# A hybrid decoder layer: the attention's squares a step later, small PSUM users in the values' bank, silu behind the weight splits, another order at v and at the scans' entry

## The chip, the cores and the metric

One core of one Trainium2 chip runs the whole layer as one program. Its engines are called here as the profile calls them: PE multiplies matrices (PEld is its weight load), DVE, ACT and POOL work on tiles in on-chip memory, SP issues the DMA transfers. The metric is the device time of one execution in microseconds. Matmul results go to PSUM, which is cut into banks; every tile in it belongs to a pool with a fixed number of buffers, and a new tile of a pool waits until the last reader of the buffer that it takes over is done.

## The reference, cut to what matters

Sixteen meta tokens are put ahead of 1024 tokens of 1024 channels. One layer computes a state-space mixer (SSD) and a stick-breaking attention side by side, projects both together, and then runs a feed-forward net with a depthwise convolution:

```python
xn = rms_norm(h, mix_pre_g)
proj = xn @ w_in                      # z, x/B/C, dt, q, k, v
xbc = silu(causal_dwconv(xbc))        # 4 taps
y_ssd = ssd_mixer(z, xbc, dt, ...)    # chunks of 128 tokens, a state passed on
# attention, 16 heads of 64:
zlog = q k^T / 8;  beta = sigmoid(zlog)
A[t,s] = beta[t,s] * prod_{s<j<t} (1 - beta[t,j])      # s < t
y_sb = rms_norm(A v, sb_norm_g)       # over all 1024 channels of a token
h = h + rms_norm(concat(y_ssd, y_sb) @ w_out)
g, u = rms_norm(h) @ w_up;  f = (gelu(causal_dwconv(g)) * u) @ w_down
return h + rms_norm(f)
```

## The kernel before, in words

All products run in a split precision: a float32 operand becomes a high part (ACT, a copy to the matmul's rounded type, `whi`, L181) and a low part (POOL, operand minus high part, `wlo`, L182), and three matmuls stand for one. The large projections use a seven-product scheme of the Strassen kind, so that sums of weight blocks are split as well (`whi4x` is the high part of the sum `s24x`).

The order of PE, DVE, ACT and POOL is the order in which the code emits instructions: the parts that matter here stand in manual schedules. SP's order is that of the DMA calls in the scans and the attention. The stages, with their times in the profile of before:

- Duos (60 to 355 us). Each duo projects two blocks of 128 channels with seven products of about 4 us (matmuls at L308). Behind each product stands a slot, into which the work on the last duo's result is put: for x, B and C four convolution taps on DVE, silu (L501) and skip (L507) on ACT, and turnings to token order in three parts (transposes to `tt_X` at L480/L485, ACT copies to `xtkX` at L481/L486). `done_conv` (L520) says which of it goes into which of the slots 0 to 9. In the same places the next duo's weights are summed and split; `split_4` (`whi4x`, then `wlo4x`) stands just ahead of slot 5.
- v (355 to 438 us). The values by the same scheme, `VORDER` = 1, 2, 6, 7, 5, 4, 3, each product in two halves s = 0, 1 over four token blocks t. The sums of weight blocks (`v_sum`, L792) run on DVE and POOL during product 2, the splits (`vwhi` L727, `vwlo` L728) follow. `v_tail` (L840) adds 64 small matmuls.
- Scans (438 to 595 us). 18 units of the state-space mixer with much waiting between engines. Between their parts the last q and k projections are run as filling (`pj_q`, `pj_k`, L218): `scan_fill` is called 54 times and gives out `SCAN_FILL` steps per 27 calls. A finished q/k piece `st` (three buffers, ACT L921 and DVE L927) is put on a list `stores`; `put_stores` issues what stands on it, and is called when the next piece is finished.
- Attention (595 to 885 us). Eight passes p, one per pair of heads, of four steps m. A step loads q blocks on SP, forms scores `z` (L1279, L1280 sigmoid on ACT), runs the products along the keys as scans on DVE (`kp`, L1285), turns earlier scans (`tw` L1303, ACT copy `th` L1308) and multiplies still earlier ones with the values (`av` L1323, ACT copy to `ysc` L1327). `do` fills in matmuls of the output projection (`mo`, L1471). PSUM pool `zz` has three buffers, shared by z, tw, `twc` (corner transposes, `edge_turn`), `halo` (rows for the output projection) and `pta` (norm sums); pool `av` has one, and uses its columns 0:2, at m = 2 also 2:4.
- At m = 2 of pass p, `edge_mix` closes pass p−1: DVE adds the tail from `av` to `ysc` (L1352), then ACT squares the finished `ysc` (`sqb`, L1359), then POOL adds that to the sum of squares `sq` (L1360). `sqb` takes a `th` buffer. In m = 3 and m = 0, `load_v` fetches the next pass's values and a shifted copy `w` (one buffer); POOL subtracts (L1220) in two parts of 5 and 4 blocks.
- Then the output projection, the feed-forward net, and the final norm (885 to 1697 us).

Of the kernel before, what the change touches and what calls it, by code (L numbers as in the profile page):

```python
# [9 lines left out]
F32 = mybir.dt.float32  # L10
# [3 lines left out]
ALU = mybir.AluOpType  # L14
# [3 lines left out]
P = 128  # L18
# [19 lines left out]
NQA = 4  # L38
SCAN_FILL = 41
FILLS = (4,) + 8 * (2,) + 23 * (1,)  # L40
# [26 lines left out]
def tile_layer(ctx: ExitStack, tc: tile.TileContext, x, meta, rows, parts,  # L67
# [721 lines left out]
    nc.sync.dma_start(out=vdz[0:1], in_=vzero)  # L789
    def v_sum(dst, a, b, op, eng):  # L790
        for s in range(2):
            eng.tensor_tensor(vq[dst][s], vq[a][s], vq[b][s], op=op)  # L792

# [56 lines left out]
    def load_b12():  # L850
        xo["b12"] = x_tile(xp, "bxh", "b12rh"), x_tile(xp, "bxl", "b12rl")
        for t, d in zip(xo["b12"], b12d):
            nc.sync.dma_start(out=t.bitcast(F32), in_=d)

    for a, n in enumerate(VORDER):
        nx = VORDER[a + 1] if n != 3 else None
        for s in range(2):
            for t in range(4):
                v_product(n, t, s)
                if nx is not None and t == (3 * (1 - s) + s if n == 2 else s):  # L860
                    v_split(nx, s)
                if n == 2 and (s, t) == (0, 0):
                    v_tail()
                    v_sum((1, 1), (1, 1), (0, 1), ALU.add, nc.vector)
                    v_sum((0, 1), (0, 0), (0, 1), ALU.subtract, nc.gpsimd)
                    v_sum((0, 0), (1, 1), (0, 0), ALU.subtract, nc.vector)
                if n == 6 and (s, t) == (0, 2):
                    v_sum((1, 0), (1, 0), (0, 0), ALU.subtract, nc.gpsimd)
# [94 lines left out]

    def token_rstd(r, pool, nm, pt):
# [6 lines left out]
        nc.vector.memset(ms[:, 0:1], 1.0)  # L971
        nc.vector.tensor_scalar(ms[:2, 0:1], pt[:2, 0:1], 1.0 / D, EPS, op0=ALU.mult, op1=ALU.add)
        nc.vector.tensor_scalar(ms[:, 1:], pt[:, 1:NT + 1], 1.0 / D, EPS, op0=ALU.mult, op1=ALU.add)
        nc.gpsimd.tensor_tensor(r, ms, nhalf[:, :NT + 1], op=ALU.pow)
# [8 lines left out]
    with tc.tile_pool(name="ssd", bufs=1, side="right") as sp:  # L983
# [171 lines left out]
        nc.sync.dma_start(out=dtk, in_=dtkd)  # L1155
        load_x(*units[0])
        load_bc(*units[1])
# [9 lines left out]
        for n, (g, c) in enumerate(units):  # L1167
            if n == 12:
                for d, u in zip(vcd, (vd, vdp)):
                    nc.sync.dma_start(out=d.rearrange("(t r) c -> t r c", r=NM),  # L1170
                                      in_=u[P:].rearrange("(t r) c -> t r c", r=P)[:, :NM])
            if n in (0, 2, 6, 10):
# [80 lines left out]

    corner = []

# [92 lines left out]
    def edge_mix(p, av):  # L1348
        av = av[:, 2:4].rearrange("p a c -> p (a c)")
        ysc = ys_of.pop(p)  # L1350
        tail = ysc[:, :, 96:P]
        nc.vector.tensor_tensor(tail, av.rearrange("p (t c) -> p t c", c=32), tail, op=ALU.add)  # L1352
        stores.append((yd1[:, :, p, :].rearrange("t d c -> d t c"), ysc))
        flat = ysc.rearrange("p t c -> p (t c)")
        if p == 0:
            nc.scalar.activation(sq[:, NM:L], flat, AF.Square)
        else:
            sqt = ap.tile([P, 2, 4, P], F32, tag="th", name=f"sqb{p}", bufs=4).rearrange("p h b c -> p (h b c)")
            nc.scalar.activation(sqt, flat, AF.Square)  # L1359
            nc.gpsimd.tensor_tensor(sq[:, NM:L], sq[:, NM:L], sqt, op=ALU.add)  # L1360

# [171 lines left out]
    def halo_go(r):  # L1533
        acc = psum_zz(f"halo{r}")[:, 0, 0:256]
        for k in (2 * r, 2 * r + 1):
# [18 lines left out]
    def row():  # L1554
        run(wsteps, 1)

    extras = {(1, 0): lambda: do(4), (1, 2): lambda: load_rows(2), (2, 0): lambda: load_rows(2), (3, 2): lambda: (halo_go(0), row()),
              (4, 0): row, (4, 2): lambda: (halo_go(1), row(), load_rows(2)),
              (5, 0): lambda: (row(), load_rows(2)), (5, 2): load_y0, (6, 0): load_y0, (6, 2): lambda: halo_go(2),
              (7, 0): split_y0, (7, 2): lambda: (halo_go(3), split_y0()), (8, 2): row, (9, 2): row, (10, 2): row,  # L1560
              (11, 2): row}
# [5 lines left out]
    for step in range(4 * 8):  # L1567
# [29 lines left out]
        if p > 0 and m == 1:  # L1597
            edge = edge_turn(p - 1)
        extra(step, 2)
        if p == 7:  # L1600
            run(meta_steps, 1)
        if p == 0 and m == 1:
            run(token_rstd(r_ssd, ap, "a", psum_zz("pta")[:, 0, :]))
    while corner:
        corner_copy(*corner.pop(0))
    pair_mix(*mix.pop(0), psum_av("av32"))
    do(1)
    pair_turn(*turn.pop(0))
    do(4)
    edge = edge_turn(7)  # L1610
    av = psum_av("av33")
    pair_mix(*mix.pop(0), av, (7, edge))
    put_stores()
    run(meta_steps)
# [842 lines left out]
```

## Time and profile before

| | us |
|---|---|
| median of three runs | 1698.51 (1696.07 to 1701.05) |
| the profiled execution | 1699.53 |
| span of its profile | 1697.4 |
| PE busy in the span | 1641.2 (97%) |
| DVE, ACT, POOL busy | 1084.5, 746.4, 765.9 |
| mean granted TensorE clock | 0.989 |

The span is the time from the first to the last instruction in the profile; some 2.1 us of the profiled execution lie around it. In the profile's rows a bracket such as `[1.66 <-ACT th L1308]` behind an instruction says how long its engine stood idle before it and which instruction of which engine ended that wait. PEclk is the clock that TensorE was granted in a window, as a share of full speed. The three stages of the diff's main parts have PE busy for 286.80 of 295 us (60 to 355), 37.96 of 42 (438 to 480), and 152.22 of 160 (710 to 870).

### The profile page before, as it was taken

What the parts mean: (1) busy time and instruction counts of PE and PEld (TensorE: products, weight loads), DVE (VectorE), ACT (ScalarE), POOL (GpSimd) and SP (SyncE); (2) the same over time, 40 slices, a digit from 0 to 9 for tenths busy, and PEclk for the clock granted to TensorE, in tenths of its full rate; (3) what the DMA queues carried; (4) which work ended last, traced back from release to release, by engine and by line L of the source; (5) the groups of instructions that cost most, each with busy time, mean ns of one, the idle gap of its engine ahead of it and who ended that gap; (6) DMA issues with size and microseconds to landing.
All of it is one profiled execution on the core that took longest, in us unless ns stands there. A gap on an engine that the chain in (4) does not pass through costs nothing.

```text
span 1697.4 us, 28962 instructions
## 1 busy us (share of the span) xinstructions
PE 1641.2 (97%) x11508; PEld 1442.9 (85%) x11508; DVE 1084.5 (64%) x1253; ACT 746.4 (44%) x1094; POOL 765.9 (45%) x582
## 2 busy tenths in 40 slices
PE   6899999999999989999999999999999999999998
PEld 5899999987777888878877888999889889888887
DVE  7776644345367678877742378666665656658777
ACT  6444344332144357766644244433333333344544
POOL 3675756620276553344332012776677777300001
PEclk9999999999999999999999999999999999999999
DMA  5333334334487866453426543232222223395335
GB/s 191 145 141 114 126 125 150 126 152 136 145 227 234 257 204 198 121 150 109 125 81 212 168 154 120 91 121 94 93 94 94 94 95 113 115 328 189 99 112 186
DMA packets 164517, 247.38 MB, mean 146 GB/s; under 512 B 18487, under 2 KB 99495, under 8 KB 162702
## 3 DMA queue, kind: packets, MB, share of 16 engines
q1 hardware_dynamic: 164382, 245.53, 44.8%
q8 instruction: 91, 1.49, 0.4%
q14 instruction: 44, 0.36, 0.1%
HBM read 161.99 MB, written 83.46 MB: 145 GB/s over the span
## 4 chain that ended last, share of the span: by engine, by line
PE 81%; issue 6%; DVE 5%; POOL 3%; DMA 2%; ACT 2%; SPq 1%; POOLq 0%; DVEq 0%; ACTq 0%
PE fX L1861 10%; PE mo L1471 10%; PE dnA L2273 7%; PE fY L1861 7%; PE fA L1861 7%; PE dnB L2273 5%; DVE kp L1285 3%; PE av L1323 3%; PE z L1279 3%; PE tw L1303 2%; PE pj_k L218 2%; PE dXqk L308 2%; PE pj_q L218 2%; PE vB L811 2%; PE vA L811 2%
## 5 line engine op out<-in xcount | busy, mean ns | idle before, releaser
L1285 DVE TENSOR_TENSOR_SCAN kp<-kp,hold 128x396 f32<-128x396 f32 (+5 forms) x224 | 197.1, 949 | 43.5 <-ACT kp L1280 41.7
L182 POOL TENSOR_TENSOR wlo<-wr,whi 128x1024 fp32r<-128x1024 f32 x43 | 99.3, 2318 | 41.0 <-ACT whi L181 41.0
L2310 POOL TENSOR_TENSOR fms<-fms 128x1 f32<-128x1 f32 x8 | 2.3, 287 | 222.0 <-DMA ar<-fda 185.9
L181 ACT ACTIVATE whi<-wr 128x1024 fp32r<-128x1024 f32 x43 | 45.7, 1062 | 112.2 <-PE fX L1861 73.5
L1933 DVE SCALAR_TENSOR_TENSOR ga<-gr,pp,ga 128x1024 f32<-128x1024 f32 x44 | 69.2, 1574 | 34.0 <-ACT ga L1926 33.2
L2195 ACT ACTIVATE dh<-ar 128x512 fp32r<-128x512 f32 x77 | 48.6, 631 | 94.8 <-PE dnB L2273 44.7
L1280 ACT ACTIVATE kp<-z 128x788 f32<-128x788 f32 (+4 forms) x96 | 73.6, 835 | 23.6 <-PE z L1279 19.7
L2196 DVE TENSOR_TENSOR dl<-ar,dh 128x512 fp32r<-128x512 f32 x77 | 53.2, 691 | 47.1 <-ACT dh L2195 47.1
L1279 PE MATMUL z<-k,q 64*128 64x396 f32 (+9 forms) x672 | 68.1, 345 | 15.1 <-ACT th L1308 9.7
L1279 PEld LDWEIGHTS z<-k,q 64*128 64x128 f32 x672 | 55.4, 195 | 28.3 <-ACT th L1308 17.5
L1308 ACT ACTIVATE th<-tw 128x1024 f32<-128x1024 f32 (+2 forms) x96 | 70.7, 811 | 14.0 <-PE tw L1303 12.6
L1323 PE MATMUL av<-th,v 128*64 128x128 f32 x1152 | 72.1, 281 | 0.0
L1303 PE MATMUL tw<-ident,kp 128*128 128x128 f32 x576 | 70.0, 276 | 0.5 <-DVE kp L1285 0.5
L1323 PEld LDWEIGHTS av<-th,v 128*64 128x64 f32 x1152 | 64.4, 140 | 6.5 <-issue 4.8
L1303 PEld LDWEIGHTS tw<-ident,kp 128*128 128x128 f32 x576 | 62.4, 141 | 7.5 <-issue 6.3
L2273 PE MATMUL dnA<-dl,dh 128*128 128x512 f32 x176 | 68.6, 390 | 0.0
L2273 PE MATMUL dnA<-dh 128*128 128x512 f32 x176 | 68.6, 390 | 0.0
L2273 PE MATMUL dnA<-dh,dl 128*128 128x512 f32 x176 | 68.5, 389 | 0.0
L1994 POOL TENSOR_TENSOR al<-wr,ah 128x512 fp32r<-128x512 f32 x20 | 28.6, 1429 | 77.6 <-ACT ah L1993 77.5
L1257 POOL TENSOR_SCALAR cb<-kp 128x32 f32<-128x32 f32 x64 | 36.1, 573 | 56.0 <-DVE kp L1285 53.3
L497 DVE SCALAR_TENSOR_TENSOR cdX<-craw_x,pp,cdX 128x1040 f32<-128x1040 f32 x24 | 51.5, 2146 | 0.6
L2273 PE MATMUL dnB<-dl,dh 128*128 128x512 f32 x132 | 51.4, 390 | 0.0
(986 smaller groups left out, 6041.5 us busy)
## 6 DMA issues: line engine op xcount, KB each, us to landing
wr<-in_w_up SPq DMA_DIRECT2D x44, 512.0 KB
fds<-ga SPq DMA_DIRECT2D x44, 256.0 KB
b<-in_w_down SPq DMA_DIRECT2D x44, 256.0 KB
ar<-fds SPq DMA_DIRECT2D x44, 256.0 KB
fda<-ga SPq DMA_DIRECT2D x33, 256.0 KB
ar<-fda SPq DMA_DIRECT2D x33, 256.0 KB
k<-qkd SPq DMA_DIRECT2D x8, 1040.0 KB
q<-qkd SPq DMA_DIRECT2D x64, 128.0 KB
```

The costliest lines, as they stand in the source:

```text
L182: nc.gpsimd.tensor_tensor(l, raw, h.bitcast(F32), op=ALU.subtract)
L218: mm(acc[:, :CQ - s], a[:, k, :], b[:, k % 4, c + s:c + CQ], start=(k == 0 and j == 0), stop=(k == KB - 1 and j == 2))
L1279: mm(z[:, j, a - lo:e - lo], u[h, :], r[h, a - bases[x]:e - bases[x]], start=s_ == 0, stop=s_ == 2)
L1280: nc.scalar.activation(kp[:, :, lo:top], z[:, :, :top - lo], AF.Sigmoid, scale=-QSCALE)
L1285: nc.vector.tensor_tensor_scan(part, part, hold[:, L - last + a:L - last + e][:, ::-1], 1.0 if e == last else kp[:, j, e:e + 1], op0=ALU.m ...
L1303: nc.tensor.transpose(tw[:, j, b, :], kp[:, j, c0:c0 + P], ident)
L1308: copied[0] = nc.scalar.activation(th[:, :, :nb, :], tw[:, :, :nb, :], AF.Copy, scale=-1.0, bias=1.0).ins
L1323: mm(av[halves[j], 1 - x, :], v[:, kb, halves[j]], th[:, j, b, :], start=kb == 0, stop=kb == i)
L1471: recent[0] = mm(acc, u[:, k, :], v[:, cs], start=(k == 0 and j == 0), stop=(k == 7 and j == 2))
L1861: mm(acc[:, c, :nn], u[:, k, :], v[:, k, c0:c0 + nn], start=first and k == 0 and j == 0, stop=k == 3 and j == 2, skip_group_check=not first)
L1933: nc.vector.scalar_tensor_tensor(v, self.g[jj][:, :, i:i + 256], fconv_w[:, j, i:i + 1], v, op0=ALU.mult, op1=ALU.add)
L2273: mm(banks[BANK[n], t], u[:, 0, c], v[:, 1, :], start=(n in (1, 2, 5) and p == 0 and i == 0), stop=(p == NPR - 1 and i == 2), skip_group_c ...
```

## The change

Five places of the code are touched; no arithmetic is added or taken away.

- `done_conv`: silu and skip of the duo's second block go from slot 4 to slot 5.
- v: product 1 takes its token blocks in the order 3, 0, 1, 2; `v_tail` and the sums come one product later, and the sums go half by half (part 0 behind block 1, part 1 behind block 3); the split of product 6's first half comes one block earlier.
- Scan entry: `put_stores` is called before the loads of the second unit and in the first two units; `SCAN_FILL` is 39 instead of 41, and the first unit gets four filling steps of its own (24 matmuls) between its state matmul (`st`, L1101) and its output matmuls (`yt`, L1117); the sum of the steps stays 82.
- Attention, PSUM: `twc`, `halo` and `pta` take columns of the `av` bank instead of a `zz` buffer; two of the four `halo_go` calls come two to four steps later; the first norm's scaling of `pta` runs on ACT, its memset on POOL, both from DVE.
- Attention, order: the square and its sum are put on a list `later` and come out at m = 3, behind that step's value product.

```diff
-SCAN_FILL = 41
+SCAN_FILL, FIRST = 39, 8
...
     def done_conv(duo, blocks):
         (a, ta_), (b, tb_) = (conv_acts(*args) for args in blocks)
-        return [a[:2], a[2:4], a[4:] + b[:2], b[2:4], ta_[:1] + b[4:], ta_[1:2], ta_[2:], tb_[:1], tb_[1:2], tb_[2:]]
+        return [a[:2], a[2:4], a[4:] + b[:2], b[2:4], ta_[:1], ta_[1:2] + b[4:], ta_[2:], tb_[:1], tb_[1:2], tb_[2:]]
...
+    def v_sums(part):
+        v_sum((1, 1), (1, 1), (0, 1), ALU.add, nc.vector, part)
+        v_sum((0, 1), (0, 0), (0, 1), ALU.subtract, nc.gpsimd, part)
+        v_sum((0, 0), (1, 1), (0, 0), ALU.subtract, nc.vector, part)
+
     for a, n in enumerate(VORDER):
         nx = VORDER[a + 1] if n != 3 else None
         for s in range(2):
-            for t in range(4):
+            for t in (3, 0, 1, 2) if n == 1 else range(4):
                 v_product(n, t, s)
-                if nx is not None and t == (3 * (1 - s) + s if n == 2 else s):
+                if nx is not None and t == (2 * (1 - s) + s if n == 2 else s):
                     v_split(nx, s)
-                if n == 2 and (s, t) == (0, 0):
+                if n == 2 and (s, t) == (0, 3):
+                    v_sums(1)
+                if n == 2 and (s, t) == (0, 1):
                     v_tail()
-                    v_sum((1, 1), (1, 1), (0, 1), ALU.add, nc.vector)
-                    v_sum((0, 1), (0, 0), (0, 1), ALU.subtract, nc.gpsimd)
-                    v_sum((0, 0), (1, 1), (0, 0), ALU.subtract, nc.vector)
+                    v_sums(0)
...
-        prev = [None, None]
-        run(fill, 8)
+        run(fill, FIRST - 8)
         cur = chunk_weights(*units[0])
...
+            if n < 2:
+                put_stores()
...
             scan_fill()
+            if n == 0:
+                run(fill, 4)
...
-    def edge_turn(p):
+    def edge_turn(p, av):
         cb = edges.pop(p)
-        tw = psum_zz(f"twc{p}").rearrange("p h (b c) -> p (h b) c", c=P)
+        tw = av[:, 2:4]
...
-        if p == 0:
-            nc.scalar.activation(sq[:, NM:L], flat, AF.Square)
-        else:
-            sqt = ap.tile([P, 2, 4, P], F32, tag="th", name=f"sqb{p}", bufs=4).rearrange("p h b c -> p (h b c)")
-            nc.scalar.activation(sqt, flat, AF.Square)
-            nc.gpsimd.tensor_tensor(sq[:, NM:L], sq[:, NM:L], sqt, op=ALU.add)
+
+        def square():
...
+        later.append(square)
...
     def halo_go(r):
-        acc = psum_zz(f"halo{r}")[:, 0, 0:256]
+        acc = av[:, 2:4].rearrange("p a c -> p (a c)")
...
             pair_mix(*mix.pop(0), av, p > 0 and m == 2 and (p - 1, edge))
+            if m == 3:
+                while later:
+                    later.pop(0)()
```

`square` holds the five removed lines as they were. The `run(fill, 8)` and the `put_stores` that open the scans now stand ahead of `load_bc(*units[1])`, so FIRST − 8 = 0 steps are left behind the loads.

On ACT in the second x duo (`craw_x` and `cdX` are the convolution's input and result, `s24x` a weight sum), before:

```order
L181 ACTIVATE whi1x_1243<-wrx_811 128x8x128
L481 ACTIVATE xtkX_1247<-tt_X_0_1248 16x128
L501 ACTIVATE cdX_1184<-cdX_1184 128x1040
L507 ACTIVATE craw_x_840<-cdX_1184,pp 128x1040
L181 ACTIVATE whi4x_1279<-s24x_1148 128x8x128
L486 ACTIVATE xtkX_1247<-tt_X_1_1283 128x512
L486 ACTIVATE xtkX_1247<-tt_X_2_1314 128x512
```

The same place on ACT after the change:

```order
L181 ACTIVATE whi1x_1243<-wrx_811 128x8x128
L481 ACTIVATE xtkX_1247<-tt_X_0_1248 16x128
L181 ACTIVATE whi4x_1276<-s24x_1148 128x8x128
L486 ACTIVATE xtkX_1247<-tt_X_1_1280 128x512
L501 ACTIVATE cdX_1184<-cdX_1184 128x1040
L507 ACTIVATE craw_x_840<-cdX_1184,pp 128x1040
L486 ACTIVATE xtkX_1247<-tt_X_2_1314 128x512
```

The weight split `whi4x` and one turning copy now stand ahead of silu and skip.

On DVE in v (`vq` are weight blocks and their sums, `vwlo` low parts; numbers 3909 and 3911 are the two halves of one block), before:

```order
L792 TENSOR_TENSOR vq_3909<-vq_3909,vq_3905 128x1024
L792 TENSOR_TENSOR vq_3911<-vq_3911,vq_3907 128x1024
L792 TENSOR_TENSOR vq_3681<-vq_3909,vq_3681 128x1024
L792 TENSOR_TENSOR vq_3683<-vq_3911,vq_3683 128x1024
L728 TENSOR_TENSOR vwlo_4061<-vq_3681,vwhi_4060 128x1024
L728 TENSOR_TENSOR vwlo_4083<-vq_3683,vwhi_4082 128x1024
```

The same six on DVE after the change:

```order
L791 TENSOR_TENSOR vq_3909<-vq_3909,vq_3905 128x1024
L791 TENSOR_TENSOR vq_3681<-vq_3909,vq_3681 128x1024
L728 TENSOR_TENSOR vwlo_4052<-vq_3681,vwhi_4051 128x1024
L791 TENSOR_TENSOR vq_3911<-vq_3911,vq_3907 128x1024
L791 TENSOR_TENSOR vq_3683<-vq_3911,vq_3683 128x1024
L728 TENSOR_TENSOR vwlo_4083<-vq_3683,vwhi_4082 128x1024
```

The first half's low part now comes before the second half's sums.

On POOL in the attention, around m = 2 and m = 3 of a pass (`cb` corner copies, `yl` a split for the output projection, `meta_q` and `meta_k` the meta tokens' rows), before:

```order
L1257 TENSOR_SCALAR cb_8518<-kp_1_8625 128x2x16 x2
L1360 TENSOR_TENSOR sq<-sq,sqb_8777 128x1024
L1457 TENSOR_TENSOR yl_4_8819<-yk_4_8296,yh_4_8818 128x1024
L1257 TENSOR_SCALAR cb_8518<-kp_2_8722 128x2x16 x2
L1225 TENSOR_TENSOR meta_q<-qm_8580 64x2 x2
L1227 TENSOR_TENSOR meta_k<-k_8578 128x16
L1220 TENSOR_TENSOR v_8780<-v_8780,w_0_8783 128x640
L1257 TENSOR_SCALAR cb_8518<-kp_3_8829 128x2x16 x2
```

The same place on POOL after the change:

```order
L1271 TENSOR_SCALAR cb_8510<-kp_1_8617 128x2x16 x2
L1475 TENSOR_TENSOR yl_4_8807<-yk_4_8289,yh_4_8806 128x1024
L1271 TENSOR_SCALAR cb_8510<-kp_2_8713 128x2x16 x2
L1376 TENSOR_TENSOR sq<-sq,sqb_8876 128x1024
L1239 TENSOR_TENSOR meta_q<-qm_8572 64x2 x2
L1241 TENSOR_TENSOR meta_k<-k_8570 128x16
L1234 TENSOR_TENSOR v_8768<-v_8768,w_0_8771 128x640
L1271 TENSOR_SCALAR cb_8510<-kp_3_8817 128x2x16 x2
```

The sum of squares now stands directly ahead of the meta rows and of the values' first subtraction, where it stood a step earlier.

More of the change, by code (lines that the diff above doesn't have):

```diff
@@ L789, in tile_layer, with v_sum @@
     nc.sync.dma_start(out=vdz[0:1], in_=vzero)
-    def v_sum(dst, a, b, op, eng):
-        for s in range(2):
-            eng.tensor_tensor(vq[dst][s], vq[a][s], vq[b][s], op=op)
+    def v_sum(dst, a, b, op, eng, s):
+        eng.tensor_tensor(vq[dst][s], vq[a][s], vq[b][s], op=op)
     def v_tile(key):
@@ L857, in tile_layer @@
         for s in range(2):
[L858 removed]
+            for t in (3, 0, 1, 2) if n == 1 else range(4):
                 v_product(n, t, s)
[L860 removed]
+                if nx is not None and t == (2 * (1 - s) + s if n == 2 else s):
                     v_split(nx, s)
[L862 removed]
+                if n == 2 and (s, t) == (0, 3):
+                    v_sums(1)
+                if n == 2 and (s, t) == (0, 1):
                     v_tail()
[L864 to L866 removed]
+                    v_sums(0)
                 if n == 6 and (s, t) == (0, 2):
[L868 removed]
+                    for part in range(2):
+                        v_sum((1, 0), (1, 0), (0, 0), ALU.subtract, nc.gpsimd, part)
                 if n == 6 and (s, t) == (1, 3):
@@ L962, in tile_layer, with token_rstd @@
     qs = {}
-    def token_rstd(r, pool, nm, pt):
+    def token_rstd(r, pool, nm, pt, scalar=False):
         for t in range(NT + 1):
@@ L970, in token_rstd @@
         ms = pool.tile([P, NT + 1], F32, tag="tms", name=f"tms{nm}")
-        nc.vector.memset(ms[:, 0:1], 1.0)
-        nc.vector.tensor_scalar(ms[:2, 0:1], pt[:2, 0:1], 1.0 / D, EPS, op0=ALU.mult, op1=ALU.add)
-        nc.vector.tensor_scalar(ms[:, 1:], pt[:, 1:NT + 1], 1.0 / D, EPS, op0=ALU.mult, op1=ALU.add)
+        (nc.gpsimd if scalar else nc.vector).memset(ms[:, 0:1], 1.0)
+        for rows_, cols_ in ((slice(0, 2), slice(0, 1)), (slice(0, P), slice(1, NT + 1))):
+            if scalar:
+                nc.scalar.activation(ms[rows_, cols_], pt[rows_, cols_], AF.Copy, scale=1.0 / D, bias=EPS)
+            else:
+                nc.vector.tensor_scalar(ms[rows_, cols_], pt[rows_, cols_], 1.0 / D, EPS, op0=ALU.mult, op1=ALU.add)
         nc.gpsimd.tensor_tensor(r, ms, nhalf[:, :NT + 1], op=ALU.pow)
@@ L1156, in tile_layer @@
         load_x(*units[0])
+        prev = [None, None]
+        run(fill, 8)
+        put_stores()
         load_bc(*units[1])
@@ L1252, in tile_layer @@
     edges, ys_of = {}, {}
-    corner = []
+    corner, later = [], []
     def corner_copy(p, i, kp, m, n):
@@ L1597, in tile_layer @@
         if p > 0 and m == 1:
-            edge = edge_turn(p - 1)
+            edge = edge_turn(p - 1, av)
         extra(step, 2)
@@ L1602, in tile_layer @@
         if p == 0 and m == 1:
-            run(token_rstd(r_ssd, ap, "a", psum_zz("pta")[:, 0, :]))
+            run(token_rstd(r_ssd, ap, "a", psum_av("pta")[:, 0, :], True))
     while corner:
         corner_copy(*corner.pop(0))
-    pair_mix(*mix.pop(0), psum_av("av32"))
+    av = psum_av("av32")
+    pair_mix(*mix.pop(0), av)
     do(1)
@@ L1609, in tile_layer @@
     do(4)
-    edge = edge_turn(7)
+    edge = edge_turn(7, psum_zz("twc7").rearrange("p h (b c) -> p (h b) c", c=P))
     av = psum_av("av33")
     pair_mix(*mix.pop(0), av, (7, edge))
+    later.pop(0)()
     put_stores()
```

12 lines of the change are left out of this document (10 added, 2 removed).

## The prediction, made before the changed kernel was run

> **What bounds the kernel now.** The page comes first: span, busy shares, and the chain of work that ended last.
>
> ```profile
> span 1697.4 us, 28962 instructions
> PE 1641.2 (97%) x11508; PEld 1442.9 (85%) x11508; DVE 1084.5 (64%) x1253; ACT 746.4 (44%) x1094; POOL 765.9 (45%) x582
> PE 81%; issue 6%; DVE 5%; POOL 3%; DMA 2%; ACT 2%; SPq 1%; POOLq 0%; DVEq 0%; ACTq 0%
> ```
>
> PE is busy 97% of the span and carries 81% of the chain. The change leaves PE's matmuls as they are, so it can only win idle time of PE, some 56 us in all, or time at a lowered clock. The second view is therefore PE's waits, grouped by waiting line and releaser; only the rows of places that the diff touches are shown.
>
> ```profile
> PE z L1279 <- ACT th L1308: 9.7, 6, 2.0
> PE dXx L308 <- POOL wlo4x L182: 2.5, 2, 1.3
> PE yt L1117 <- DVE em L1081: 1.9, 1, 1.9
> PE tt_X L480 <- ACT xtkX L486: 1.4, 3, 0.7
> PE vB L811 <- DVE vwlo L728: 1.3, 1, 1.3
> PE dXqk L308 <- POOL wlo4qk L182: 1.2, 1, 1.2
> PE z L1279 <- PE z L1279: 1.1, 2, 0.8
> PE vA L811 <- DVE craw_qk L320: 0.9, 1, 0.9
> PE halo L1537 <- ACT th L1308: 0.7, 1, 0.7
> PE dXz L308 <- POOL wlo4z L182: 0.5, 1, 0.5
> PE z L1279 <- DVE mh L1542: 0.3, 1, 0.3
> ```
>
> They sum to 21.5 us: 5.6 in the duos, 2.2 at v, 1.9 at the scans' entry, 11.8 in the attention. The third view is the table of windows with the granted clock (columns: window, length, busy time and count of PE, PEld, DVE, ACT, POOL, then PEclk, DMA share, GB/s).
>
> ```profile
> 230.90:234.30 3.40, 3.40 (x18) 3.40 (x17) 0.00 (x0) 1.58 (x3) 2.69 (x3) 0.50 0.44 162
> 691.70:695.10 3.40, 1.77 (x10) 1.16 (x8) 1.68 (x3) 1.69 (x2) 0.55 (x1) 1.00 1.10 301
> 695.10:698.50 3.40, 3.07 (x41) 2.58 (x43) 0.86 (x1) 3.40 (x6) 3.25 (x6) 1.00 0.89 264
> 790.70:794.10 3.40, 1.74 (x14) 1.04 (x14) 0.39 (x2) 2.98 (x4) 1.84 (x1) 1.00 1.03 288
> 794.10:797.50 3.40, 3.40 (x30) 2.94 (x30) 1.52 (x1) 3.28 (x5) 2.74 (x2) 0.50 0.35 106
> 710.00:870.00 160.00, 152.22 (x1589) 130.75 (x1587) 123.77 (x152) 104.17 (x149) 62.14 (x68) 0.98 0.38 112
> ```
>
> The window from 790.7 has 1.66 us of PE idle, and the next is granted half the clock; a like window at 691.7 was not followed by one. A wait of this size so sometimes costs a second time.
>
> **Duos.** The rows are ACT and POOL in the second x duo.
>
> ```profile
> 224.46 1.07 ACT L501 ACTIVATE cdX<-cdX 128x1040 f32<-128x1040 f32 x1 [4.80 <-DVE cdX L497]
> 226.63 1.05 ACT L181 ACTIVATE whi4x<-s24x 128x1024 fp32r<-128x1024 f32 x1
> 227.76 2.17 POOL L182 TENSOR_TENSOR wlo4x<-s24x,whi4x 128x1024 fp32r<-128x1024 f32 x1 [4.43 <-ACT whi4x L181]
> ```
>
> ACT stood idle 4.80 us until DVE's last tap let silu start, then did silu and skip (to 226.63) and only then `whi4x`; POOL, idle 4.43 us, ended `wlo4x` at 229.93, and PE waited. After the change `whi4x` runs inside ACT's idle time and `wlo4x` ends before 227, ahead of PE's first need near 228. One turning copy moves up as well; silu itself starts when DVE lets it, as before, and the last copy follows skip at 226.7, where `tt_X` needs its bank at 227.5. Late next is thus that copy, with under 1 us in hand. Gain 5.6 us. The clock window from 230.9 follows these two waits (0.7 and 1.3 us) and holds 3.4 us of work that would take 1.7 at full clock: gain 1.7. **Duos −7.3**, between −7.3 and −3.0 (a third of the waits and the clock window stay).
>
> **v.** Product 1 begins with block 3, whose bank is not that of the duos' last eviction: the 0.9 us wait on `craw_qk` goes; nothing hides in it that another block would bring. The sums start one product later, split in halves. The window row (PE alone) gives PE's pace, 44 matmuls in 10 us, 0.23 for one.
>
> ```profile
> 356.00:366.00 10.00, 10.00 (x44) 1.00 0.61 224
> 367.95 3.79 PE L840 MATMUL vtail<-vq,xtail 128*16 128x256 f32 x64
> 370.83 2.36 DVE L792 TENSOR_TENSOR vq<-vq,vq 128x1024 f32<-128x1024 f32 x2 [4.14 <-PE vtail L840]
> 379.06 6.58 POOL L792 TENSOR_TENSOR vq<-vq,vq 128x1024 f32<-128x1024 f32 x2 [1.25 <-PE vA L811]
> 380.02 6.70 DVE L728 TENSOR_TENSOR vwlo<-vq,vwhi 128x1024 fp32r<-128x1024 f32 x2
> ```
>
> A sum takes DVE 1.2 us alone and 3.35 while POOL works on its own (380.02), POOL 2.4 to 3.3. Now in order: `vtail` at 368.6 (six matmuls of 0.23 later than the 367.95 of before, less the 0.9), first DVE sum 2.9 behind it as before, 371.5, POOL's first 372.7 to 375.0, DVE's next to 376.2, high part 1.1, low part to 378.5, so the first half is early and the 1.3 us wait on `vwlo` goes. The second half: DVE's sum to 379.7, POOL's to 382.5, then DVE's last sum beside POOL's next one (3.4) to 385.9, high part to 387.0, low part 2.4 to 389.4. PE asks for it at about 387.0: `vtail`, 36 + 24 more matmuls, and the third of the next block. A new wait of 2.4 us: behind it stand all of PE's later products. **v −0.9 −1.3 +2.4 = +0.2**; between −2.2 (DVE undisturbed: ready at 386.1) and +3 (with a half-clock window).
>
> **Scan entry.** A piece `st` had to wait for a buffer.
>
> ```profile
> 456.92 0.39 ACT L921 ACTIVATE st<-pj_q 128x260 fp32r<-128x260 f32 x1 [6.99 <-DMA qkd<-st]
> ```
>
> The stores that free the buffers stood on SP behind the loads of two units; ACT's mask work (`em`) stood behind this piece, and PE's `yt` behind `em`. With stores ahead of the loads ACT doesn't wait. The loads move back by two or three SP issues of 0.4 to 0.6 us (rows of SP further down), an estimate of 1.2 us; `yt` comes about 1.1 us later than before, but 24 filling matmuls stand ahead of it that are no longer done elsewhere. They take 2.8 us: −1.7. A half-clock window there gets shorter, an estimate of 0.6. **−2.3**, between −4 and +1 (the loads' delay shows and the wait stays). The two steps fewer per 27 calls are the same matmuls at another place.
>
> **Attention: what goes.** The rows are PE's score products and ACT's square.
>
> ```profile
> 760.57 2.21 PE L1279 MATMUL z<-k,q 64*128 64x396 f32 x24 [1.66 <-ACT th L1308]
> 775.88 1.89 PE L1279 MATMUL z<-k,q 64*128 64x456 f32 x18
> 793.14 3.15 PE L1279 MATMUL z<-k,q 64*128 64x396 f32 x24 [1.66 <-ACT th L1308]
> 791.12 1.06 ACT L1359 ACTIVATE sqb<-ysc 128x1024 f32<-128x1024 f32 x1 [2.71 <-DVE ysc L1352]
> ```
>
> At 788.4 (791.12 − 2.71) ACT had `tw` to copy, but the square stood first in its queue and waited 2.71 us for DVE's tail, which stands behind the step's scans. Deferred, it leaves the first `th` free to start when its transposes are done, some 2 us earlier, and z, which asked at 791.48, has its bank: six waits, −9.7. Halo, corner and norm sums leave the three-buffer pool: −0.7 −1.1 −0.3. The moved memset and scaling and the later halo calls lie beside filled PE time: 0. The clock: the 24 matmuls of z took 3.15 us in the half-clock window and 2.21 outside it, and the mean of 0.98 over the 160 us of the table's last row is 3.2 us of full clock missing, two such windows behind these waits: −3.2.
>
> At m = 3 the square costs ACT 1.06 us ahead of `th`; z of m = 0 by the steps' spacing still finds its bank free, with some 0.9 us in hand: 0. `sqb` keeps its place among the four `th` buffers.
>
> **Attention: what comes.** The sum of squares on POOL now stands ahead of the values' subtraction; the rows are POOL's and SP's.
>
> ```profile
> 759.69 2.38 POOL L1360 TENSOR_TENSOR sq<-sq,sqb 128x1024 f32<-128x1024 f32 x1 [8.08 <-ACT sqb L1359]
> 764.29 2.02 POOL L1220 TENSOR_TENSOR v<-v,w 128x640 f32<-128x640 f32 x1
> 769.21 1.29 POOL L1220 TENSOR_TENSOR v<-v,w 128x512 f32<-128x512 f32 x1 [0.74 <-DMA w<-vd]
> 766.34 0.36 SPq L1216 DMA_DIRECT2D w<-vd  x1
> 767.32 1.18 SPq L960 DMA_DIRECT2D q<-qkd  x2
> ```
>
> Count from the start of z at m = 3 (760.57). Before, the subtraction ended at +5.7; SP, which has the second load of `w` in its queue (one buffer), went on at +5.8, and the q blocks of m = 1 behind it went out at +6.75 for a need at +15.3. After: scores and value product 2.2 each to +4.4, its copy +4.8, square to +5.9, sum of squares beside DVE's scans 3.2 (the 640 columns took 2.02, so 1024 take 3.2) to +9.1, meta rows and subtraction 3.9 (762.07 to 766.31 before, less a corner copy) to +13.0. SP then issues `w` in two parts and the first q at +14.0. A transfer lands about 2 us after its issue (the last part of `w`, issued by 767.3, let POOL go at 769.21): +16.0 to 16.6, for a need at +15.3. A wait of about 0.9 us in the five passes that have both: **+4.5**, between 0 and 5 × 2.5. [...]
>
> The corner transposes wait for the `av` bank's last reader, done before they start; the next value product waits for the corner's DVE reads:
>
> ```profile
> 783.67 0.76 DVE L1338 TENSOR_TENSOR thc<-twc,cmask 128x256 f32<-128x256 f32 x2 [0.37 <-PE twc L1335]
> 785.36 2.19 PE L1323 MATMUL av<-th,v 128*64 128x128 f32 x36
> ```
>
> They ended at 784.43, 0.93 ahead of it: 0. **Attention −9.7 −2.1 −3.2 +4.5 = −10.5**, between −15 and −3.
>
> **Sum.** −7.3 + 0.2 − 2.3 − 10.5 = −19.9. The profiled execution took 1699.5 (span 1697.4 and 2.1 around it), 1.0 above the median: 1679.6 by it, 1678.6 by the median; I say **1679**.
>
> **Rivals.** *The path over POOL, SP and q takes back what the square freed.* For it: DVE's scans slow the sum of squares, and the lag adds up; against: at m = 1 the rest of the queue is short. With 2.7 us in five passes the attention gives −1.5: 1688. *The waits move.* DVE is busy 123.77 of 160 us between 710 and 870, and more by share once the waits go; if the scans end last, `tw` waits for `kp` where z waited for `th`. Attention ±0, v at +3, half the duos' gain, the scans' entry at −1: 1698.5 + 3 − 3.6 − 1 = 1697. *The half clock isn't tied to these waits.* The row at 691.7 speaks for it, those at 230.9 and 790.7 against. Then the waits go and three windows stay, 1.7 + 3.2 = 4.9: 1684. [...] *The one `av` bank.* Every value product of m = 2 now stands behind the corner's reads on DVE, which stand behind scans; in hand are 0.93 us in seven passes. If DVE comes to them 5 us later, 7 × 4.1 = 28.5 are lost: 1707, slower. It decides from 3.8 us lateness (0.93 + 19.9 / 7).
>
> **How the numbers follow.** Forecast 0.55; POOL and q 0.17; clock 0.12; waits move 0.10; `av` bank 0.06. Below 1693.4 or above 1703.6 (0.3%, about what a measurement of this kernel can tell from no change) counts as faster or slower. Forecast, POOL and clock are faster, 0.84; the moved waits mostly same, 0.09; the bank slower, with a rest, 0.07. The range: low end 1669 (v −2.2, scan entry −4, attention −15, duos −7.3, sum −28.5, and 1 for the runs' spread), high end 1694, which takes in the POOL rival with v at +3, a clock window and the same spread; the upper parts of the last two rivals are left out.
>
> **What would show it.** Right: `whi4x` ahead of silu and no wait of PE on `wlo4x`; no wait of z on `th`, `th` 2 us earlier at m = 2; PE waiting on `vwlo` once for about 2 us; ACT's `st` at the entry without a wait; SP's `w` load about 7 us later at m = 3, and z waiting for q about 0.9 us at m = 1; no half clock at 230.9 and between 710 and 870. Wrong: `av` waiting for `thc`, `tw` for `kp`, z for q by more than 2 us.

## The result, and the profile after

The changed kernel takes 1685.39 us (median of 4; 1682.9 to 1688.21) against 1698.74 for the kernel before: a ratio of 0.9922, 95% interval 0.99 to 0.9945, so 13.4 us less. The forecast was 1679 in a range of 1669 to 1694. The profiled execution of the changed kernel is its fastest, 1682.9; that of the kernel before, 1699.53, lies 0.8 above its median. The two profiles therefore differ by more (16.3 us of span) than the medians do.

The page's first lines, after:

```profile
span 1681.1 us, 28980 instructions
PE 1635.2 (97%) x11508; PEld 1442.2 (86%) x11508; DVE 1092.0 (65%) x1250; ACT 746.6 (44%) x1096; POOL 779.8 (46%) x583
```

PE's waits, after, grouped by waiting line and releaser (total, times, longest), at v and the scans:

```profile
PE vB L810 <- DVE vwlo L728: 1.7, 1, 1.7
PE sg L1059 <- DMA sg<-diagd: 1.5, 1, 1.5
PE vB L810 <- ACT vwhi L727: 0.7, 1, 0.7
PE yt L1130 <- DVE yt L1105: 0.4, 1, 0.4
```

The same view of the same kernel, cut to 620 to 870 us, its two rows:

```profile
PE z L1293 <- DMA q<-qkd: 7.7, 5, 2.2
PE av L1337 <- PE z L1293: 0.5, 1, 0.5
```

The waits on `wlo4`, `xtkX`, `craw_qk`, `em`, on `th` and in the three-buffer pool are all gone. New are 7.7 us of z on q, in five places, 2.4 us at v (0.7 for a high part, 1.7 for a low part) and 1.5 us at `sg` (0.3 before). One wait of z on q in the first pass (3.0 us before, 2.0 after) stands in both kernels. From the starts of the first matmul of each stage in both traces (the last row ends at the feed-forward net's first `fX`):

| stage (us) | before | after | measured | forecast |
|---|---|---|---|---|
| duos | 293.1 | 283.3, with 0.9 of v's gain | −8.9 | −7.3 |
| v | 90.4 | 93.1 | +2.7 −0.9 = +1.8 | +0.2 |
| scans | 150.1 | 149.6 | −0.5 | −2.3 |
| attention to the feed-forward net | 494.5 | 485.3 | −9.2 | −10.5 |

The four stages give −16.8 in this pair of profiles (what lies outside them is 0.5 us longer), and the medians −13.4, for a forecast of −19.9.

In the duos, the rows of ACT and POOL in the second x duo:

```profile
217.74 1.06 ACT L181 ACTIVATE whi4x<-s24x 128x1024 fp32r<-128x1024 f32 x1 [1.23 <-PE dYz L308]
220.75 1.07 ACT L501 ACTIVATE cdX<-cdX 128x1040 f32<-128x1040 f32 x1 [1.47 <-DVE cdX L497]
219.57 3.21 POOL L182 TENSOR_TENSOR wlo4x<-s24x,whi4x 128x1024 fp32r<-128x1024 f32 x1
```

`whi4x` now runs 3 us ahead of silu, in time in which ACT had idled, and `wlo4x` ends at 222.78, before PE's first use of it at 224.59.

In the attention, PE, POOL and SP from m = 3 of the fifth pass to m = 1 of the sixth:

```profile
746.03 2.04 PE L1293 MATMUL z<-k,q 64*128 64x396 f32 x24
763.41 2.87 PE L1293 MATMUL z<-k,q 64*128 64x456 f32 x14 [2.17 <-DMA q<-qkd]
751.64 3.11 POOL L1376 TENSOR_TENSOR sq<-sq,sqb 128x1024 f32<-128x1024 f32 x1 [5.88 <-ACT sqb L1375]
757.30 2.30 POOL L1234 TENSOR_TENSOR v<-v,w 128x640 f32<-128x640 f32 x1
759.63 0.37 SPq L1230 DMA_DIRECT2D w<-vd  x1
760.63 1.19 SPq L965 DMA_DIRECT2D q<-qkd  x2
```

From z of m = 3 at 746.03: the sum of squares from +5.6 to +8.7, the subtraction to +13.6, SP's `w` at +13.6, q at +14.6, z of m = 1 at +17.4 where PE had asked at +15.2.

### The profile page after: what moved, and what is told of

Same layout as the page of the kernel before. It is cut to its first block, busy times and chain, and to the rows that moved or that the text cites. A ratio compares the mean times of both kernels' runs of the same rounds, so it can differ in the third digit from the quotient of the medians.

```text
span 1681.1 us, 28980 instructions
## 1 busy us (share of the span) xinstructions
PE 1635.2 (97%) x11508; PEld 1442.2 (86%) x11508; DVE 1092.0 (65%) x1250; ACT 746.6 (44%) x1096; POOL 779.8 (46%) x583
## 4 chain that ended last, share of the span: by engine, by line
PE 53%; DMA 0%; POOL 0%; ACT 0%; SPq 0%; issue 0%; DVE 0%; DVEq 0%; POOLq 0%; ACTq 0%
PE fX L1885 10%; PE mo L1489 9%; PE dnA L2297 7%; PE fY L1885 7%; PE fA L1885 7%; PE dnB L2297 5%; PE av L1337 2%; PE tw L1317 1%; PE z L1293 1%; PE g0a L1899 1%; DMA q<-qkd 0%; PE x2tp L1763 0%; PE g0d L1899 0%; PE g0c L1899 0%; PE u0a L1899 0%; PE u0d L1899 0%
## 5 line engine op out<-in xcount | busy, mean ns | idle before, releaser
L1299 DVE TENSOR_TENSOR_SCAN kp<-kp,hold 128x396 f32<-128x396 f32 (+5 forms) x224 | 211.5, 1015 | 30.6 <-ACT kp L1294 28.7
L1271 POOL TENSOR_SCALAR cb<-kp 128x32 f32<-128x32 f32 x64 | 39.9, 632 | 56.4 <-DVE kp L1299 45.2
L2297 PE MATMUL dnB<-dh,dl 128*128 128x512 f32 x132 | 51.4, 389 | 0.0
L2297 PE MATMUL dnB<-dh 128*128 128x512 f32 x132 | 51.4, 389 | 0.0
```

Source lines behind the costliest of these rows:

```text
L1299: nc.vector.tensor_tensor_scan(part, part, hold[:, L - last + a:L - last + e][:, ::-1], 1.0 if e == last else kp[:, j, e:e + 1], op0=ALU.m ...
L2297: mm(banks[BANK[n], t], u[:, 0, c], v[:, 1, :], start=(n in (1, 2, 5) and p == 0 and i == 0), stop=(p == NPR - 1 and i == 2), skip_group_c ...
```

## The experiments

**The parts alone.** Four kernels, each the kernel before with one part of the change; then the attention's part cut in two. The edits are the hunks shown with the change, so only some lines of each are repeated. Ratios are to the kernel before as it ran beside each kernel (medians 1699.87 to 1701.1); differences of medians from different sets of runs carry that shift of 1 to 2 us as well.

Duos:

```diff
-... b[2:4], ta_[:1] + b[4:], ta_[1:2], ta_[2:], ...
+... b[2:4], ta_[:1], ta_[1:2] + b[4:], ta_[2:], ...
```

> The kernel before with the change of done_conv alone. Theory: the waits of PE on wlo4x, wlo4z, wlo4qk and xtkX go (5.6 us of idle in the duos), the half-clock window at 230.9 with them (1.7), and each removed wait gives back a little more than its idle time, since a lone matmul shows 0.28 us where the pace is 0.12: v starts 8.5 to 9.5 us earlier than in the kernel before (355.23), and nothing after that changes by more than 2 us: 1689 to 1691. Rival: the gain in the duos depends on the other parts or is lost to other waits later: v starts 8.5 us earlier, but the total is within 4 us of the kernel before, 1695 or more.

1690.35 us, ratio 0.9937 (0.9915 to 0.9959). v starts 8.7 us earlier, and 8.1 of that are left at the end of the span. The theory holds.

v:

```diff
-            for t in range(4):
+            for t in (3, 0, 1, 2) if n == 1 else range(4):
...
+                    v_sums(1)
```

> The kernel before with the changes at v alone (block order of product 1, vtail and sums later and by halves). Theory: PE waits for the parts of product 6's second half, 2.4 us, where before it waited 1.3 us for the first half; the 0.9 us wait on craw_qk goes; with a half-clock window behind it v ends 0 to 2 us later than before: 1697 to 1701. Rival: by halves is better and the changed kernel's 2.4 us wait comes from the shifted phase of other work: v ends 2 us earlier, 1696.

1700.72 us, ratio 1.0002 (0.9988 to 1.0016): no difference. The same two waits stand in its profile (0.7 and 1.7 us), and no half-clock window behind them. From the first duo to `sg` it takes 383.6 us, as before: the old waits are gone and the new ones stand in their place. This part is worth nothing alone; the wait belongs to the new order and not to the phase of other work.

Scan entry:

```diff
-SCAN_FILL = 41
+SCAN_FILL, FIRST = 39, 8
...
+            if n < 2:
+                put_stores()
...
+            if n == 0:
+                run(fill, 4)
```

> The kernel before with the changes at the scans' entry alone. Theory: the wait of yt (1.9 us) goes, but the loads of sg, now behind the stores on SP, come later, PE waits for them about 1.5 us instead of 0.3, and half-clock windows remain around: the attention starts 0 to 1 us earlier: 1697.5 to 1698.7. Rival: the 0.5 us that the changed kernel gained there is what is left after a loss elsewhere in its scans that this kernel doesn't have: attention 2 us earlier, 1696.5.

1698.14 us, ratio 0.9987 (0.9973 to 1.0002). In its profile the attention starts 1.4 us earlier than before, between theory and rival; `sg` waits 0.8 us and `yt` 0.6 and 0.5. The total is not clear of its noise.

The attention, whole:

```diff
+        later.append(square)
...
-        acc = psum_zz(f"halo{r}")[:, 0, 0:256]
+        acc = av[:, 2:4].rearrange("p a c -> p (a c)")
```

> The kernel before with all changes in the attention and none elsewhere. Theory: six waits of z on th (9.7) and the four small ones (2.1) go, z waits for q at m = 1 in five passes, 7 to 8 us in all; from the first z to the start of the feed-forward net 9 us less than before (494.5): 1689 to 1691. Rival: the waits for q come from the phase that the earlier stages give the DMA queues, not from the attention's own order: here less than 3 us of them, 1685 or less.

1691.1 us, ratio 0.9946 (0.9928 to 0.9964). From the first z to the feed-forward net 484.7 us, 9.8 less than before; z waits for q here too, 8.7 us with the old wait of the first pass (2.1). The waits come from the attention's own order.

The four ratios add up to 1.28% (21.8 us), the whole change gives 0.78% (13.3). In the profiles the parts give −8.8, 0.0, −1.4 and −9.8, together −20.0 for −16.8: the whole has a half-clock window at v that the part alone did not have (1.7), and 1.0 less at the scans' entry and 0.6 less in the attention. That explains the profiles; what else separates the medians stays open.

The deferred square alone:

```diff
+            if m == 3:
+                while later:
+                    later.pop(0)()
```

> The kernel before with the deferred square alone; corners, halo rows and norm sums stay in the three-buffer pool. Theory: the waits of z on th at m = 3 go, the waits of z on q at m = 1 come (about 7 us in five passes), because POOL's sum of squares now ends before the values' subtraction and SP's load of w with it: total gain over before 2 to 6 us. Rival (the bank move is what shifts q): no waits on q, gain 9 us or more.

1692.96 us, ratio 0.996 (0.9947 to 0.9974), some 7 us less. PE's waits between 620 and 880 us:

```profile
PE z L1279 <- DMA q<-qkd: 6.8, 5, 1.9
PE z L1279 <- PE z L1279: 1.1, 2, 0.8
PE z L1279 <- DVE mh L1546: 0.2, 1, 0.2
```

The waits on `th` are gone and five waits on q have come: both sides of the change hang on the square. The gain is 1 us above the end of what was expected.

The bank moves alone (`twc`, `halo`, `pta` in `av`'s columns, two halo calls one step later each, from steps 6 and 7 to 7 and 8, and not two to four steps as the list of changes has it; the square at m = 2):

```diff
-        tw = psum_zz(f"twc{p}").rearrange("p h (b c) -> p (h b) c", c=P)
+        tw = av[:, 2:4]
```

> The kernel before with the bank moves alone (corners, halo rows, norm sums in the values' bank, later halo calls); the square stays at m = 2. Theory: the six waits of z on th stay at about 1.7 each, no waits on q at m = 1, the small waits (2.1 us) go: gain 1 to 4 us. Rival: the three-buffer pool was what z waited for, and with the corner out of it z has its buffer: the waits on th go as well, gain 8 us or more.

1701.67 us, ratio 1.0007 (0.9994 to 1.0021). The same view, 620 to 890 us:

```profile
PE z L1282 <- ACT th L1311: 11.9, 7, 2.2
PE av L1326 <- PE z L1282: 0.5, 1, 0.5
```

No gain, where 1 to 4 us were expected; the rival is refuted as well: with the corner out of the three-buffer pool z still waits for `th`, once more and 2.2 us longer in sum.

**What holds q.** The changed kernel with only POOL's addition moved behind the subtraction:

```diff
-                nc.gpsimd.tensor_tensor(sq[:, NM:L], sq[:, NM:L], sqt, op=ALU.add)
+                adds.append(lambda: nc.gpsimd.tensor_tensor(sq[:, NM:L], sq[:, NM:L], sqt, op=ALU.add))
...
             if m > 1:
                 next(vsteps, None)
+        while adds:
+            adds.pop(0)()
```

> The changed kernel with POOL's sum of squares emitted behind the values' subtraction of m = 3; ACT's square stays where the change put it. Theory: the subtraction ends 3 us or more earlier, SP's load of w and q with it, z's waits on q at m = 1 go: 7 to 8 us less than the changed kernel, 1676 to 1679; POOL's corner copies come 3 us later, which the corner transposes two steps on do not feel. Rival: q is late because SP's loads stand in its queue behind the store of y or the loads of w and k, whatever POOL does: 1 us or less.

1676.76 us, ratio 0.9864 (0.9847 to 0.9882), 8.6 us below the changed kernel's median, 9.8 by the two ratios, whose intervals lie apart. Its timeline has POOL in the fourth pass and SP in the fifth:

```profile
721.57 1.71 POOL L1234 TENSOR_TENSOR v<-v,w 128x640 f32<-128x640 f32 x1
723.24 3.06 POOL L1376 TENSOR_TENSOR sq<-sq,sqb 128x1024 f32<-128x1024 f32 x1
...
750.01 0.37 SPq L1230 DMA_DIRECT2D w<-vd  x1
751.00 1.19 SPq L965 DMA_DIRECT2D q<-qkd  x2
```

And all waits of PE in it from 620 to 870 us:

```profile
PE av L1337 <- PE z L1293: 1.0, 2, 0.7
PE mo L1489 <- DVE ysc L1366: 1.0, 1, 1.0
PE av L1337 <- DVE thc L1352: 0.4, 2, 0.2
PE av L1337 <- DVE mh L1560: 0.2, 1, 0.2
```

Both kernels start z of m = 3 of the fifth pass near 746 (745.88 and 746.03); q goes out 5.1 us behind it instead of 14.6, and in this stretch no z waits for it. The path from POOL over SP's queue to q is shown. The corner's wait (`av` on `thc`, 0.4 us) appears for the first time here: the one bank does cost, but little.

**v.** The changed kernel with the sums and `vtail` as before, product 1's block order kept:

```diff
-                if n == 2 and (s, t) == (0, 3):
-                    v_sums(1)
-                if n == 2 and (s, t) == (0, 1):
+                if n == 2 and (s, t) == (0, 0):
                     v_tail()
-                    v_sums(0)
+                    v_sum((1, 1), (1, 1), (0, 1), ALU.add, nc.vector)
+                    v_sum((0, 1), (0, 0), (0, 1), ALU.subtract, nc.gpsimd)
+                    v_sum((0, 0), (1, 1), (0, 0), ALU.subtract, nc.vector)
```

> The changed kernel with the sums and vtail at v as before (whole sums behind the first product), and product 1's block order 3, 0, 1, 2 kept. Theory: PE waits for vwlo of the first half as before, 1.3 us, and not for the second: v ends 1 to 3 us earlier than in the changed kernel (93.1 us from its start to the scans' first sg): 1682.5 to 1684.5. Rival: product 1's block order delays the old sums just as much, and the new placement was needed for it: no less, 1685 or more.

1682.84 us, ratio 0.9908 (0.988 to 0.9935). v takes 91.5 us instead of 93.1. But v still starts 1.0 us earlier than without the block order and takes 1.0 longer than before (`vtail` waits 0.6 us for weights): the block order gives nothing in the sum. Between the totals the intervals overlap.

With POOL's addition behind the subtraction, and both halves of DVE's first sum ahead of the second:

```diff
     def v_sums(part):
-        v_sum((1, 1), (1, 1), (0, 1), ALU.add, nc.vector, part)
+        for both in range(2 * (part == 0)):
+            v_sum((1, 1), (1, 1), (0, 1), ALU.add, nc.vector, both)
```

> The changed kernel with POOL's sum of squares behind the values' subtraction (as in the kernel of that name before) and, at v, both halves of DVE's first sum ahead of its second, so that POOL's second half needn't wait for DVE's low part of the first half. Theory: POOL's second half then ends near 368.3 instead of 373.1, DVE's last sum and the split follow 4 us earlier, PE's waits at product 6 (0.7 and 1.7 us) go, with them the half-clock window behind: from v's start to the scans' first sg 90 us instead of 93.1, total 1673 to 1675. Rival: the long sum is DVE beside POOL's next one, whatever the order, and the waits stay: 1676 to 1678.

1674.31 us, ratio 0.9852 (0.9837 to 0.9866). The total is as the theory had it, its reason only half. POOL, DVE and PE there:

```profile
365.42 5.68 POOL L791 TENSOR_TENSOR vq<-vq,vq 128x1024 f32<-128x1024 f32 x2 [8.69 <-DVE vq L791]
368.77 3.41 DVE L791 TENSOR_TENSOR vq<-vq,vq 128x1024 f32<-128x1024 f32 x1 [2.29 <-POOL vq L791]
375.87 0.50 PE L810 MATMUL vB<-vwlo,t2h 128*128 128x512 f32 x1 [1.81 <-DVE vwlo L728]
```

The long sum is now the first half's, beside POOL's second (3.41 us, 1.2 alone), and PE waits 1.8 us for the first half instead. The rival named that. The wait of 0.7 and the half clock are gone (v 90.9 us), but the half clock only by the place of the windows (last section): in the next kernel but one, with the same code at v, it is back and v takes 92.4 us.

POOL's addition behind the subtraction together with the old sums, the edits of the two runs above that have one of them each:

> The same with POOL's sum of squares behind the subtraction, but v with whole sums behind the first product as in the kernel before (product 1's block order 3, 0, 1, 2 kept). Theory: as in the run with these sums and without the POOL change, from v's start to the first sg 91 to 91.5 us, one wait of 1.2 us on vwlo stays without a half-clock window: 1674 to 1676, within 2 us of the kernel with both first sums ahead. Rival: part of what that run gained lay in the attention, by the phase of its waits on q, and is gone with them: 1677 or more.

1674.56 us, ratio 0.985 (0.9835 to 0.9865), v 91.1 us with one wait of 1.1: no different from the other form.

**The scans' entry.** The kernel with both first sums ahead, the second unit's `sl` and `sg` loads ahead of the stores:

```diff
         run(fill, 8)
-        put_stores()
         load_bc(*units[1])
+        put_stores()
```

> The kernel with both first sums ahead and POOL's sum of squares behind, and at the scans' entry the stores behind the sl and sg loads of the second unit instead of ahead of them. Theory: PE's wait on sg (1.4 us) goes or falls under 0.5, the stores go out 1.2 us later and the pieces still find a buffer, as 24 matmuls stand ahead of yt: the attention starts 1 to 2 us earlier than without it. Rival: the piece that the mask work stands behind waits for its buffer again, and what sg gains yt loses: within 0.5 us at the start of the attention.

1674.31 us, ratio 0.985 (0.983 to 0.987). One of its four executions took 6947.67 us, for a reason that no trace shows; the ratio leaves it out, and the other three have a median of 1673.14. `sg` no longer waits for its load, but `yt` now waits 1.2 us for 0.4, so that a part of the wait has moved, as the rival said. From v's start to the attention 239.6 us pass instead of 241.6, with half clock for 3.4 us at v and none at the scans' entry, where the kernel without this edit had 10.2 us of it: how much of the 2 us is the wait and how much the clock, these two traces can't tell. The total does not show it.

The same edit of the entry with v's old sums and POOL's addition behind the subtraction, all that was found together:

> The kernel with POOL's sum of squares behind the subtraction and v's whole sums, and the scans' stores behind the second unit's sl and sg loads. Theory: its wait on sg (1.1 us) goes as it did with the other form of v, the start of the attention moves 1 us earlier or a little more, total 1672.5 to 1674.5. Rival: the wait moves to yt and the total stays, 1674 to 1675.5.

1671.53 us, ratio 0.984 (0.9826 to 0.9853), 13.9 us below the changed kernel. Its windows table has, for the scans' entry (44 us; in the kernel before and after, the clock was 0.92 and 0.91 from 438 or 440 to 480):

```profile
436.00:480.00 44.00, 43.05 (x324) 33.77 (x325) 17.88 (x35) 16.09 (x27) 23.49 (x24) 1.00 0.73 193
```

No half clock is left there. `sg` doesn't wait for its load and `yt` waits 0.4 us. It came out 1 us below what was expected. From v's start to the attention it takes 237.4 us, 1.7 less than the same kernel without the edit of the entry; that kernel had one half-clock window there (447.54), worth as much, and the intervals of the two totals overlap. So the wait is shown to go, a gain in time is not.

## Why the prediction was right in the main, and where its steps failed

The direction, the range and the order of the terms were right, and so were the two mechanisms that carried them: work of ACT standing ahead of a split or a copy that PE needs, and POOL's sum on the way to q. The gain forecast was 19.9 and the medians' is 13.4; the result lies between the forecast (1679) and the first rival (1688), which priced the same path at 2.7 us a pass; it took 1.5. Part of the closeness is luck: the duos gave 1.6 us more than forecast, about what v lost to a half-clock window.

- *Attention, what comes: +4.5 forecast, 7.7 measured.* The step that failed is the landing, "about 2 us after its issue". It was counted from 767.3, when SP had gone on to q, to POOL's release; from the start of `w`'s issue the same rows give 2.87 us (766.34 to 769.21). From the start of q's issue to z it is 2.8 us (760.63 to 763.41). q's issue also came at +14.6 for +14.0: the sum of squares ended earlier than forecast, at +8.7 for +9.1 (it took 2.6 to 3.1 us in the five passes, beside DVE's scans, for 3.2; in the kernel before, with DVE idle beside it, 2.4 each time), but the meta rows and the subtraction behind it took 4.9 us for 3.9 in the fifth pass. Five times the 0.8 of the landing is 4.0, more than the 3.2 missing: the waits run from 0.9 to 2.2, and in the fourth pass, the one with 0.9, POOL's meta rows took 1.6 us where they took 2.6 in the fifth. A wait of z on q by more than 2 us was named as a sign of being wrong; one of the five, 2.17, reached it.
- *Attention, what goes: −9.7 and the pools' −2.1.* All six waits on `th` went. Of the small ones 0.5 us stayed, as `av` behind z. Of the two half-clock windows one came back at 763.46, behind the 2.17 us wait on q.
- *v: +0.2 forecast, +1.8 measured.* The wait itself was exact, 2.4 us (0.7 + 1.7). What the sum left to the range's upper end is the half-clock window behind it (381.16, worth 1.7); the kernel with v's part alone had the same two waits, no such window, and neither gained nor lost (0.0). The rows of DVE and POOL, after:

```profile
369.40 1.22 DVE L791 TENSOR_TENSOR vq<-vq,vq 128x1024 f32<-128x1024 f32 x1
370.70 4.75 POOL L791 TENSOR_TENSOR vq<-vq,vq 128x1024 f32<-128x1024 f32 x2 [4.83 <-DVE vq L791]
373.13 3.40 DVE L791 TENSOR_TENSOR vq<-vq,vq 128x1024 f32<-128x1024 f32 x1 [2.51 <-POOL vq L791]
```

  POOL idles 4.83 us until DVE has done the first half's low part and then the second half's first sum, and DVE's last sum is stretched to 3.40: the chain as forecast.
- *Scan entry: −2.3 forecast, −0.5 measured.* ACT's piece no longer waits for a store, and `yt` waits 0.4 us for 1.9. The step that failed is the loads' delay: the sum put it at 1.2 us and let it show in `yt` alone, 1.1 us later, and had no term for `sg`, whose load moved back too. SP and PE after:

```profile
443.93 0.29 SPq L1029 DMA_DIRECT2D sg<-diagd  x1
446.63 0.63 PE L1059 MATMUL sg<-sg,sl 32*16 32x512 f32 x2 [1.46 <-DMA sg<-diagd]
```

  PE uses the load 2.7 us after the start of its issue, and stood still for 1.46 of them. The half clock, forecast to get shorter, stayed 6.8 us long in sum (449.43 and 459.67). With these two loads ahead of the stores the wait on the load went.
- *Duos: −7.3 forecast, −8.9 measured.* The waits and the clock window went as said. The term is too small in part because an idle time counts from the modelled end of the last matmul. PE before, around one wait:

```profile
227.16 0.28 PE L308 MATMUL dAx<-b11l,whi1x 128*128 128x260 f32 x1
227.27 0.28 PE L308 MATMUL dAx<-b11h,wlo1x 128*128 128x260 f32 x1
228.21 0.28 PE L480 MATMUL tt_X<-ident,cdX 128*16 128x128 f32 x1 [0.66 <-ACT xtkX L486]
```

  From start to start 0.94 us pass where the pace, from one matmul's start to the next, is 0.12: the wait costs 0.82 and not 0.66. Seven such waits are 1.1 of the 1.6 us; the rest is open.
- *Rivals.* No wait moved to DVE's scans and none to the corner, so the two dear rivals were rightly small. Of the three half-clock windows priced, two went with their waits and one came back behind a longer wait (last section), so the rival that keeps all three falls. That the medians differ by some 3 us less than the profiles is because the profiled execution of the changed kernel is 2.5 below its median and that of the kernel before 0.8 above its own; why executions of one kernel differ by 5 us and more was not settled.

## What to carry to other kernels

When a step is moved, follow the in-order queue that it lands in to the end: here an addition on POOL, off every critical path, held a buffer, that buffer held a load on SP, and behind that load stood the one that PE needed (q went out 14.6 us behind z's start, and 5.1 with the addition behind the subtraction). Price a transfer from the start of its issue to the first instruction that used it (q 2.8 us, `sg` 2.7), and a PE wait from start to start less the pace (0.82 us where the idle time shows 0.66). Ask for each new wait of 1.6 us or more whether it also costs a clock window, as the counts below show it can (1.7 us, half of a window of 3.41). And don't count the parts' gains as the whole's: here the parts alone add up to more than the change gave.

## What the runs showed of the hardware

In most places of these traces the half clock follows idle time within one window of a fixed grid. Edges of the granted clock lie 3.413 us or multiples of it apart within an execution (in the traces of before and after alike, the half clock lasts 3.413 or 6.827 us at each of the seven places ahead of the span's end), and the grid's place in the span differs from trace to trace (the first half-clock window, ahead of all code that an edit touches, starts between 19.98 and 22.76 us). Windows on that grid (columns: window, length, PE busy and count, PEclk, DMA share, GB/s), after:

```profile
377.75:381.16 3.41, 1.67 (x6) 1.00 0.64 243
381.16:384.57 3.41, 3.41 (x10) 0.50 0.49 154
695.21:698.62 3.41, 1.74 (x10) 1.00 0.51 139
698.62:702.03 3.41, 3.19 (x44) 1.00 0.96 313
760.07:763.48 3.41, 1.24 (x8) 1.00 0.74 171
763.48:766.89 3.41, 3.41 (x20) 0.50 0.84 291
```

and the same wait at v in the kernel with v's changes alone, with no half clock:

```profile
388.73:392.14 3.41, 1.68 (x8) 1.00 0.54 189
392.14:395.55 3.41, 3.41 (x17) 1.00 0.39 144
```

With PE idle for 1.74 us of a window (3.41 less 1.67) the next was halved, with 1.67 (695.21) and 1.73 (388.73) it was not: these numbers, in which the ends of matmuls are modelled, show no sharp border. Over all traces of this case, leaving out the first 60 us, the last 20 (where two windows with 1.86 and 1.87 us of idle were not followed by half clock) and the two places with very small matmuls (440 to 465, 598 to 622), 14 of 14 windows at full clock with 1.75 us of idle or more were followed by half clock, 15 of 23 between 1.6 and 1.75, and 1 of 87 between 0.9 and 1.5 (in the traces of before and after alone 2 of 2, 3 of 5 and 0 of 14). Idle time is not the whole of it: in the two places left out the half clock also followed windows with 0.0 and 0.6 us of visible idle (456.26 and 446.02 after) and 0.8 (452.79 before), and near 94 us, behind a run of 18 matmuls of 16 columns (2.09 us from 91.39 before), it came with none at all in every trace but one; why was not tested. The same code can fall either way: the two kernels with both halves of DVE's first sum ahead are alike up to the scans' entry and wait 1.8 us at v. In the one with the stores behind the loads, all 1.82 us lie in the window from 372.86, and the next is halved; in the other an edge at 375.27 cuts the wait into 1.2 and 0.6, and no window is halved. So the wait of 1.8 us cost another 1.7 (half of a full window of 3.41) where it lay in one window, and nothing more where an edge cut it.
